# A hybrid mixer trunk on one core: a 128-column GLA state, norm factors spread by transposes, the heads' scale on the outputs, and the channel mixer's carry tile made last

## The chip, the cores and the metric

One Trainium2 chip, of which the kernel uses one core. The metric is the device time in microseconds of one execution. TensorE is called PE here, VectorE DVE, ScalarE ACT, GpSimdE POOL, and SyncE, which issues the DMAs, SP.

## The reference

One layer of a decoder trunk over 2048 tokens of width 1024, float32 throughout.

```python
def reference(x, c, ...):
    mod = silu(c) @ w_ada + b_ada                  # sh1, sc1, g1, sh2, sc2, g2
    h = rms_norm(x) * (1 + sc1) + sh1
    x = x + g1 * token_mixer(h)
    h = rms_norm(x) * (1 + sc2) + sh2
    x = x + g2 * conv_ffn(h)                       # up-projection, causal conv of width 3, silu gate, down-projection
    return rms_norm(x) * final_gain

def token_mixer(h):
    proj = h @ w_in                                # q, k, v and gates of three groups of heads
    o_r = rms_norm(retention(q_r, k_r, v_r)) * silu(gate_r)     # 4 heads, fixed decays
    o_h = rms_norm(gated_state(q_h, k_h, v_h, log_f)) * silu(gate_h)   # 8 HGRN2 heads, 64 keys each
    o_a = rms_norm(gated_state(q_a, k_a, v_a, g_log)) * silu(gate_a)   # 4 GLA heads, 32 keys each
    return (concat(o_r, o_h, o_a) * head_gain) @ w_out

# gated_state, in chunks: S is the state of one head (keys x 64 values)
#   o = attn @ v + (q * exp(cum)) @ S
#   S = exp(last) * S + (k * exp(last - cum)).T @ v
```

## The kernel before

The tokens are worked off in four blocks of 512, each of four chunks of 128 tokens. In a block the units run in the order h0, g, h1, h2, h3, r0, r1: two HGRN2 heads to each h, all four GLA heads in g (as two subs), two retention heads to each r. Each unit projects its q, k, v and gate out of h with float32 weights that are split into a high and a low half (three matmuls for one), builds the attention in seven levels (`gated`), copies, transposes k, updates its state and multiplies (`attn_out`). Each pair of heads' output is then transposed (`transposed`), and split into halves too. `out_half(b, 0)` multiplies the first four of these eight outputs with the out-projection at the end of the block; `out_finish(b - 1)` does the second four after unit h0 of the next block, and takes the second norm. This mixer takes the first 1290 us; then the channel mixer runs as up- and down-products over two halves of the tokens.

The order on PE is written out by hand: a clock in the program (`clock`, `adv`, `clock.at`) counts the PE time that each step is thought to take, and steps that fall due are put in between. The orders on DVE, ACT and SP come from a scheduler that goes by priorities (`tc.high_priority`) and by the program's order. Tiles come from rings of buffers: whoever takes a buffer again waits for its last reader.

What the change touches:
- `piece` brings in one 512 KB piece of weights: raw data into the ring `wraw` of two buffers (NRAW), a high half `whi` by ACT, a low half `wlo` by DVE. Low halves are written to a scratch in DRAM (`keep`) in block 0 and read back later. Pieces of the out-projection are multiplied by the heads' scale in this step (`gain`), in four parts of 256 columns, and for them the high half is kept and read back as well. The same two raw buffers also take the adaLN weights (`wada`), which DVE works off one at a time between the pieces (`ada`, from the list `later`).
- `rstd` spreads a norm factor, one number for each token, over all partitions: a matmul of the factor as a broadcast with the identity (`second`). The startup and the last norm have a copy of that line.
- `states` holds for each unit the states of five chunks, 128 columns wide with two heads on the block diagonal, but 64 wide for the GLA unit (i == 4), whose four heads stand on 32 partitions each, one above the other.
- `attn_out` adds, for each chunk, the two heads' attention times v (64 columns each) and q times the state. With `qn`, a copy of the two heads' q in one tile, that is one matmul of 128 columns; without it (GLA) each head's q, zero elsewhere (`new_qbd`, three buffers that POOL zeroes), is multiplied with the state on its own.
- `m_all` is the mask for the copies of levels 1 to 16.
- `halo` carries the last two columns of the convolution's input from one half of the tokens to the other; it is the first tile of the pool `gemm`.

In the rows below, names carry the block first: rhqh is the raw piece for the q of an HGRN2 unit, hhqh and lhqh its high and low half, pshfh and pshqh the projections into PSUM, ha the high and low halves of the normed input, xn its unsplit form, bcn the spread norm factor, og, oh, or the outputs of a unit, oTg, oTh, oTr their transposes, ath and qbh the attention and the q of an h unit, hwo and lwo a piece of the out-projection.

Of the kernel before, what the change touches and what calls it, by code (L numbers as in the profile page):

```python
# [9 lines left out]
F32 = mybir.dt.float32  # L10
F32R = mybir.dt.float32r
I32 = mybir.dt.int32
U32 = mybir.dt.uint32
AF = mybir.ActivationFunctionType
ALU = mybir.AluOpType
# [85 lines left out]
def trunk(ctx, tc, xT, vecs, cvec, cst, rope, msk, wada, win, walow, wgla, wout, wup, wdown, out):  # L101
# [41 lines left out]
    m_all = p1.tile([P, 448], U32, tag="msk", name="m_all")  # L143
# [68 lines left out]
    def piece(src, name, key, gain=None, ahead=50):  # L212
# [3 lines left out]
        with tc.high_priority(offset=ahead):  # L216
            hi = pw.tile([P, 1024], F32R, tag="whi", name="h" + name)
            lo = pw.tile([P, 1024], F32R, tag="wlo", name="l" + name)
            if key + "h" in kept:
                nc.sync.dma_start(hi[:].bitcast(F32), kept[key + "h"][:])  # L220
                nc.sync.dma_start(lo[:].bitcast(F32), kept[key + "l"][:])
                return hi, lo
            raw = pw.tile([P, 1024], F32, tag="wraw", name="r" + name, bufs=NRAW)
            nc.sync.dma_start(raw[:], src)
            if gain is None:
                S.copy(hi[:], raw[:])
                if key + "l" in kept:
                    nc.sync.dma_start(lo[:].bitcast(F32), kept[key + "l"][:])
                else:
                    V.tensor_tensor(lo[:], raw[:], hi[:], op=ALU.subtract)  # L230
                    keep(key + "l", lo[:])
            else:
                n = 1024 // len(gain)
                for i, g in enumerate(gain):
                    sl = slice(i * n, (i + 1) * n)
                    S.activation(hi[:, sl], raw[:, sl], AF.Copy, scale=g)
                for i, g in enumerate(gain):
                    sl = slice(i * n, (i + 1) * n)
                    V.scalar_tensor_tensor(lo[:, sl], raw[:, sl], g, hi[:, sl], op0=ALU.mult, op1=ALU.subtract)
                keep(key + "h", hi[:])  # L240
                keep(key + "l", lo[:])
# [76 lines left out]
    def rstd(acc, name, bc, then, bank=None, gap=4.5):  # L318
# [13 lines left out]
        def second(r):  # L332
            p = bank("bc" + name)
            for c in range(NCH):
                T.matmul(p[:, c * P:(c + 1) * P], r[:, c:c + 1].to_broadcast([P, P]), ident, start=True, stop=True)
            S.copy(bc, p[:])
            then()
# [38 lines left out]
    def startup():  # L376
# [48 lines left out]
        for c in range(NCH):  # L425
            T.matmul(ps[:, c * P:(c + 1) * P], r[:, c:c + 1].to_broadcast([P, P]), ident, start=True, stop=True)
# [87 lines left out]
    states = [p1.tile([P, NS, 64 if i == 4 else P], F32, tag=f"S{i}", name=f"S{i}") for i in range(7)]  # L514
    for i, st in enumerate(states):
        if i != 4:
            G.memset(st[:], 0.0)
# [37 lines left out]
    def transposed(b, pos, o, name):  # L555
# [5 lines left out]
        S.copy(oT[:, 0, :], ps[:])  # L561
        V.tensor_tensor(oT[:, 1, :], ps[:], oT[:, 0, :], op=ALU.subtract)
        oTs[b][pos] = oT

    def attn_out(name, b, attn, v, q, Sst, qn=None):

        ps = late_ps("o" + name)
        for c in range(NCH):
            oc = ps[:, c * P:(c + 1) * P]
            cs = slice(c * P, (c + 1) * P)  # L570
            inter = not (b == 0 and c == 0)
            both = inter and qn is not None
            st = Sst[:, (b * NCH + c) % NS, :]
            if both:
                T.matmul(oc, qn[:, cs], st, start=True, stop=False)
            for hh in range(2):
                oo = oc[:, hh * 64:hh * 64 + 64]
                T.matmul(oo, attn[:, (c * 2 + hh) * P:(c * 2 + hh + 1) * P], v[:, c, hh * 64:hh * 64 + 64],
                         start=not both, stop=hh == 1 if both else not inter)
                if inter and not both:  # L580
                    T.matmul(oo, q[:, hh, cs], st, start=False, stop=True)
# [16 lines left out]
    def gated(name, b, ui, pos, kq, decay, subs, qk, sel):  # L598
# [16 lines left out]
        for li, s in enumerate(LEVELS):  # L615
# [9 lines left out]
            with tc.high_priority(offset=CHAIN):  # L625
# [7 lines left out]
                for ps, at in zip(pss, attns):  # L633
# [5 lines left out]
                    else:  # L639
                        mk = m_all[:, li * 64:li * 64 + 64].rearrange("p (n s) -> p n s", s=s)  # L640
# [3 lines left out]
        qn = None  # L644
# [4 lines left out]
        with tc.high_priority(offset=CHAIN):  # L649
            S.copy(kT[:].rearrange("p c n -> p (c n)"), ps[:])  # L650
            if not two:
                q, rows = subs[0][:2]
                qn = late("qn" + name)
# [884 lines left out]
```

## Time and profile before

| | |
|---|---|
| runs | 3 |
| median, lowest, highest | 2593.47, 2592.66, 2594.07 us |
| span of the profiled execution | 2594.1 us, 0.6 above the median |
| busy: PE, DVE, ACT, POOL | 97%, 77%, 43%, 6% |
| DMA | 533.89 MB, 60.4% of the 16 engines' time |

The profile shows one execution by engine, line and time. A group's row gives the line, the engine, what is written and read, the shape, the count, and the durations; matmuls are pipelined, so what a matmul costs is read from the distance between starts, not from its duration. A timeline's row gives start and duration in us, and in brackets how long the engine was idle just before, and what released it. In the chain of work that ended last, each piece is followed back to what released it.

### The profile page before, as it was taken

What the parts mean: (1) busy time and instruction counts of PE and PEld (TensorE: products, weight loads), DVE (VectorE), ACT (ScalarE), POOL (GpSimd) and SP (SyncE); (2) the same over time, 40 slices, a digit from 0 to 9 for tenths busy, and PEclk for the clock granted to TensorE, in tenths of its full rate; (3) what the DMA queues carried; (4) which work ended last, traced back from release to release, by engine and by line L of the source; (5) the groups of instructions that cost most, each with busy time, mean ns of one, the idle gap of its engine ahead of it and who ended that gap; (6) DMA issues with size and microseconds to landing.
All of it is one profiled execution on the core that took longest, in us unless ns stands there. A gap on an engine that the chain in (4) does not pass through costs nothing.

```text
span 2594.1 us, 37215 instructions
## 1 busy us (share of the span) xinstructions
PE 2525.0 (97%) x13198; PEld 2141.8 (83%) x13198; DVE 1991.7 (77%) x3650; ACT 1116.4 (43%) x1898; POOL 144.6 (6%) x246
## 2 busy tenths in 40 slices
PE   5999999999999999999999999999999999999998
PEld 4798878998889888998778888878878888888887
DVE  8778986868778786887688888886677778778566
ACT  3333434433343234333254445455444455455442
POOL 1000010000000000000010000000000001010000
PEclk9999999999999999999999999999999999999999
DMA  8543556765687846887665444477675544447663
GB/s 302 194 156 131 213 215 225 276 214 179 218 311 262 294 166 222 298 280 252 204 233 173 149 144 161 146 268 242 204 228 167 154 143 145 154 132 258 207 188 126
DMA packets 232778, 533.89 MB, mean 206 GB/s; under 512 B 25072, under 2 KB 28176, under 8 KB 232592
## 3 DMA queue, kind: packets, MB, share of 16 engines
q1 hardware_dynamic: 232592, 531.52, 60.4%
q8 instruction: 104, 1.70, 0.3%
q14 instruction: 82, 0.67, 0.1%
HBM read 397.72 MB, written 133.69 MB: 205 GB/s over the span
## 4 chain that ended last, share of the span: by engine, by line
PE 85%; DVE 7%; DMA 4%; ACT 2%; issue 1%; SPq 0%; DVEq 0%; ACTq 0%
PE X L246 6%; PE X L248 6%; PE X L247 6%; PE lvh L622 3%; PE Z L247 3%; PE Z L246 3%; PE Z L248 3%; PE dX L248 3%; PE dX L246 3%; PE dX L247 3%; PE psqkvgr L248 2%; PE psqkvgr L246 2%; PE psqkvgr L247 2%; PE y L246 2%; PE y L248 2%; PE y L247 2%
## 5 line engine op out<-in xcount | busy, mean ns | idle before, releaser
L246 PE MATMUL X<-B,A 128*128 128x512 f32 x572 | 224.9, 393 | 1.4 <-ACT u L1245 1.4
L247 PE MATMUL X<-B,A 128*128 128x512 f32 x572 | 224.3, 392 | 0.3 <-DMA B<-made 0.2
L248 PE MATMUL X<-B,A 128*128 128x512 f32 x572 | 224.4, 392 | 0.0
L973 DVE TENSOR_TENSOR dA<-rd,dA 128x512 fp32r<-128x512 f32 x154 | 106.0, 689 | 94.4 <-ACT dA L972 93.9
L972 ACT CAST dA<-rd 128x512 fp32r<-128x512 f32 x154 | 95.4, 619 | 147.1 <-PE dY L248 47.3
L973 DVE TENSOR_TENSOR A<-s,A 128x512 fp32r<-128x512 f32 x176 | 120.4, 686 | 42.6 <-ACT A L972 42.4
L246 PE MATMUL psvgh<-hvgh,ha 128*128 128x256 f32 x480 | 140.3, 292 | 0.0
L248 PE MATMUL dX<-dB,dA 128*128 128x512 f32 x352 | 139.0, 395 | 0.0
L246 PE MATMUL dX<-dB,dA 128*128 128x512 f32 x352 | 139.0, 395 | 0.0
L247 PE MATMUL dX<-dB,dA 128*128 128x512 f32 x352 | 138.9, 395 | 0.0
L247 PE MATMUL psvgh<-lvgh,ha 128*128 128x256 f32 x480 | 136.0, 283 | 0.0
L248 PE MATMUL psvgh<-hvgh,ha 128*128 128x256 f32 x480 | 136.0, 283 | 0.0
L972 ACT CAST A<-s 128x512 fp32r<-128x512 f32 x176 | 108.3, 617 | 62.2 <-PE Z L248 47.5
L246 PEld LDWEIGHTS X<-B,A 128*128 128x128 f32 x572 | 107.7, 188 | 25.6 <-ACT u L1245 2.2
L247 PEld LDWEIGHTS X<-B,A 128*128 128x128 f32 x572 | 107.7, 188 | 24.4 <-DMA B<-made 1.3
L248 PEld LDWEIGHTS X<-B,A 128*128 128x128 f32 x572 | 107.6, 188 | 23.4
L246 PE MATMUL Z<-B,A 128*128 128x512 f32 x308 | 121.7, 395 | 2.3 <-ACT B L972 1.7
L622 PEld LDWEIGHTS lvh<-qbh,kh 128*128 128x128 f32 x896 | 115.8, 191 | 7.8 <-issue 1.4
L247 PE MATMUL Z<-B,A 128*128 128x512 f32 x308 | 121.5, 395 | 0.3 <-DVE B L973 0.3
L248 PE MATMUL Z<-B,A 128*128 128x512 f32 x308 | 121.6, 395 | 0.0
L622 PE MATMUL lvh<-qbh,kh 128*128 128x128 f32 x896 | 120.8, 277 | 0.3 <-DVE kh L632 0.3
L973 DVE TENSOR_TENSOR A<-r,A 128x512 fp32r<-128x512 f32 x130 | 89.3, 687 | 32.2 <-ACT A L972 32.2
(453 smaller groups left out, 7149.3 us busy)
## 6 DMA issues: line engine op xcount, KB each, us to landing
gs<-yv SPq DMA_DIRECT2D x154, 256.0 KB, 2.9
rb<-gs SPq DMA_DIRECT2D x154, 256.0 KB, 4.0
r<-wup SPq DMA_DIRECT2D x141, 256.0 KB, 3.3
s<-sumsu SPq DMA_DIRECT2D x132, 256.0 KB, 3.0
wada<-wada SPq DMA_DIRECT2D x48, 512.0 KB, 4.8
rd<-sumsd SPq DMA_DIRECT2D x88, 256.0 KB, 3.9
rd<-wdown SPq DMA_DIRECT2D x66, 256.0 KB, 3.7
x<-xT SPq DMA_DIRECT2D x64, 256.0 KB, 5.1
```

Source lines behind the costliest of these rows:

```text
L246: T.matmul(ps, lhs[0], rhs[0], start=first, stop=False, skip_group_check=more)
L247: T.matmul(ps, lhs[0], rhs[1], start=False, stop=False, skip_group_check=more)
L248: T.matmul(ps, lhs[1], rhs[0], start=False, stop=last, skip_group_check=more)
L622: T.matmul(ps[:, c * P:(c + 1) * P].rearrange("p (h n s) -> p h n s", h=2, s=s), kq[:, c * P:(c + 1) * P], rhs, start=True, stop=True)
L972: S.copy(hi, src)
L973: V.tensor_tensor(lo, src, hi, op=ALU.subtract)
```

## The change

- The GLA unit's state becomes 128 columns wide, with two heads on the block diagonal as for the other units, and is zeroed at the start. In `gated` the second head's q is copied beside the first one's in the same tile, for all units, and `attn_out` multiplies it with the state in one matmul of 128 columns. The tile `qn` of the h units is gone: their matmul reads q itself.
- The norm factors are spread by transposes in place of matmuls, in all three places.
- The out-projection's weights are no longer multiplied by the heads' scale. Its high halves are cast from raw in every block, like those of the other pieces, and only the low halves are kept. The scale goes onto the transposed outputs, where they are split.
- The mask is loaded as 256 columns and one column in sixteen of the next 64; level 16 reads that column as a broadcast.
- `halo` is made when it is first used, as the last tile of its pool.

```diff
@@ the mask
-    m_all = p1.tile([P, 448], U32, tag="msk", name="m_all")
+    m_all = p1.tile([P, 260], U32, tag="msk", name="m_all")
...
-    nc.sync.dma_start(m_all[:], msk)
+    nc.sync.dma_start(m_all[:, 0:256], msk[:, 0:256])
+    with nc.allow_non_contiguous_dma("one column in sixteen of the mask"):
+        nc.sync.dma_start(m_all[:, 256:260], msk[:, 256:320:16])
...
-                        mk = m_all[:, li * 64:li * 64 + 64].rearrange("p (n s) -> p n s", s=s)
+                        if s < 16:
+                            mk = m_all[:, li * 64:li * 64 + 64].rearrange("p (n s) -> p n s", s=s)
+                        else:
+                            mk = m_all[:, 256:260].unsqueeze(2).to_broadcast([P, nb, s])
@@ piece
-    def piece(src, name, key, gain=None, ahead=50):
+    def piece(src, name, key, ahead=50):
...
-            if key + "h" in kept:
-                nc.sync.dma_start(hi[:].bitcast(F32), kept[key + "h"][:])
-                nc.sync.dma_start(lo[:].bitcast(F32), kept[key + "l"][:])
-                return hi, lo
             raw = pw.tile([P, 1024], F32, tag="wraw", name="r" + name, bufs=NRAW)
             nc.sync.dma_start(raw[:], src)
-            if gain is None:
-                S.copy(hi[:], raw[:])
-                if key + "l" in kept:
-                    nc.sync.dma_start(lo[:].bitcast(F32), kept[key + "l"][:])
-                else:
-                    V.tensor_tensor(lo[:], raw[:], hi[:], op=ALU.subtract)
-                    keep(key + "l", lo[:])
+            S.copy(hi[:], raw[:])
+            if key + "l" in kept:
+                nc.sync.dma_start(lo[:].bitcast(F32), kept[key + "l"][:])
             else:
-                n = 1024 // len(gain)
-                for i, g in enumerate(gain):
-                    sl = slice(i * n, (i + 1) * n)
-                    S.activation(hi[:, sl], raw[:, sl], AF.Copy, scale=g)
-                for i, g in enumerate(gain):
-                    sl = slice(i * n, (i + 1) * n)
-                    V.scalar_tensor_tensor(lo[:, sl], raw[:, sl], g, hi[:, sl], op0=ALU.mult, op1=ALU.subtract)
-                keep(key + "h", hi[:])
+                V.tensor_tensor(lo[:], raw[:], hi[:], op=ALU.subtract)
                 keep(key + "l", lo[:])
@@ second, in rstd; the same line in startup and in the last norm
-                T.matmul(p[:, c * P:(c + 1) * P], r[:, c:c + 1].to_broadcast([P, P]), ident, start=True, stop=True)
+                T.transpose(p[:, c * P:(c + 1) * P], r[:, c:c + 1].to_broadcast([P, P]), ident)
@@ states
-    states = [p1.tile([P, NS, 64 if i == 4 else P], F32, tag=f"S{i}", name=f"S{i}") for i in range(7)]
-    for i, st in enumerate(states):
-        if i != 4:
-            G.memset(st[:], 0.0)
+    states = [p1.tile([P, NS, P], F32, tag=f"S{i}", name=f"S{i}") for i in range(7)]
+    for st in states:
+        G.memset(st[:], 0.0)
@@ transposed
-        S.copy(oT[:, 0, :], ps[:])
-        V.tensor_tensor(oT[:, 1, :], ps[:], oT[:, 0, :], op=ALU.subtract)
+        hg = vec[:, V_HG + pos:V_HG + pos + 1]
+        S.activation(oT[:, 0, :], ps[:], AF.Copy, scale=hg)
+        V.scalar_tensor_tensor(oT[:, 1, :], ps[:], hg, oT[:, 0, :], op0=ALU.mult, op1=ALU.subtract)
@@ attn_out
-    def attn_out(name, b, attn, v, q, Sst, qn=None):
+    def attn_out(name, b, attn, v, qn, Sst):
...
-            both = inter and qn is not None
-            st = Sst[:, (b * NCH + c) % NS, :]
-            if both:
-                T.matmul(oc, qn[:, cs], st, start=True, stop=False)
+            if inter:
+                T.matmul(oc, qn[:, c * P:(c + 1) * P], Sst[:, (b * NCH + c) % NS, :], start=True, stop=False)
...
-                if inter and not both:
-                    T.matmul(oo, q[:, hh, cs], st, start=False, stop=True)
@@ gated
             S.copy(kT[:].rearrange("p c n -> p (c n)"), ps[:])
-            if not two:
-                q, rows = subs[0][:2]
-                qn = late("qn" + name)
-                for hh, (r0, r1) in enumerate(rows):
-                        S.copy(qn[r0:r1, :], q[r0:r1, hh, :])
+            for q, rows, v, sg in subs:
+                r0, r1 = rows[1]
+                S.copy(q[r0:r1, 0, :], q[r0:r1, 1, :])
...
-                        es = slice(0, 64) if two else slice(64 * hh, 64 * hh + 64)
+                        es = slice(64 * hh, 64 * hh + 64)
...
-            ps = attn_out(f"{name}_{i}", b, at, v, q, Sst, qn)
+            ps = attn_out(f"{name}_{i}", b, at, v, q[:, 0, :], Sst)
@@ the gemm pool (halo[:, t, :] becomes halo(t) where it is used)
-    halo = pg.tile([P, 2 * NF + 4, 2], F32, tag="halo", name="halo")
+    halos = []
+
+    def halo(t):
+        if not halos:
+            halos.append(pg.tile([P, 2 * NF + 4, 2], F32, tag="halo", name="halo"))
+        return halos[0][:, t, :]
```

PE's order stays the same apart from the rows below. For GLA unit 0 of block 0 (og: its first output; S: the state, vg: v, atg: the attention, qbg: q) PE has before:

```order
L248 MATMUL psvgh_2_0_1572<-hvgh_2_1_1663,ha_7_636 128x256
L578 MATMUL og_0_1685<-vg_0_855,atg_0_1150 128x64 x3
L581 MATMUL og_0_1685<-S_111,qbg_0_848 128x64
L578 MATMUL og_0_1685<-vg_0_855,atg_0_1150 128x64
L581 MATMUL og_0_1685<-S_111,qbg_0_848 128x64
```

and after:

```order
L233 MATMUL psvgh_2_0_1572<-hvgh_2_1_1665,ha_7_637 128x256
L559 MATMUL og_0_1687<-vg_0_857,atg_0_1150 128x64 x2
L557 MATMUL og_0_1687<-S_111,qbg_0_850 128x128
L559 MATMUL og_0_1687<-vg_0_857,atg_0_1150 128x64 x2
L557 MATMUL og_0_1687<-S_111,qbg_0_850 128x128
L559 MATMUL og_0_1687<-vg_0_857,atg_0_1150 128x64 x2
```

Of the first chunk, which has no state yet, nothing changes; each later chunk has one matmul of 128 columns ahead of the two with v, in place of one of 64 behind each.

On DVE at the turn from block 0 to block 1 (wada: the adaLN weights that stand in a raw buffer; omsr, orsr, nw: the norm of unit r0 and its Newton steps; S_113: the state of unit r1), before, around the adaLN step and, some 60 rows later, around the last xn and ha:

```order
L352 SCALAR_TENSOR_TENSOR xn_1_2753<-xn_1_2753,mod,bc_1_1855 128x512
L197 ISA wada_3105,mod<-wada_3105,c_act,vec 128x1024
L197 ISA mod 128x1
...
L158 SCALAR_TENSOR_TENSOR orsr_0_3143<-nw,orsr_0_3143 128x8
L352 SCALAR_TENSOR_TENSOR xn_7_2789<-xn_7_2789,mod,bc_1_1855 128x512
L156 SCALAR_TENSOR_TENSOR nw<-orsr_0_3143 128x8
L562 TENSOR_TENSOR oTh_3_0_3162<-oTh_3_0_3157,oTh_3_0_3162 128x512
L157 TENSOR_TENSOR nw<-nw,omsr_0_3140 128x8
L197 ISA wada_3214,mod<-wada_3214,c_act,vec 128x1024
L197 ISA mod 128x1
L158 SCALAR_TENSOR_TENSOR orsr_0_3143<-nw,orsr_0_3143 128x8
L359 SCALAR_TENSOR_TENSOR ha_7_2792<-xn_7_2789,mod,ha_7_2792 128x512
```

and after:

```order
L337 SCALAR_TENSOR_TENSOR xn_6_2775<-xn_6_2775,mod,bc_1_1851 128x512
L337 SCALAR_TENSOR_TENSOR xn_7_2781<-xn_7_2781,mod,bc_1_1851 128x512
L843 TENSOR_TENSOR or_0_3094<-or_0_3082,c_all 128x512
L344 SCALAR_TENSOR_TENSOR ha_6_2778<-xn_6_2775,mod,ha_6_2778 128x512
L344 SCALAR_TENSOR_TENSOR ha_7_2784<-xn_7_2781,mod,ha_7_2784 128x512
L532 TENSOR_REDUCE omsr_0_3098<-osqr_0_3096 128x8
...
L822 SCALAR_TENSOR_TENSOR S_113<-S_113,c_all,ur_1_3138 64x64
L158 SCALAR_TENSOR_TENSOR orsr_0_3101<-nw,orsr_0_3101 128x8
L197 ISA wada_3063,mod<-wada_3063,c_act,vec 128x1024
L197 ISA mod 128x1
L156 SCALAR_TENSOR_TENSOR nw<-orsr_0_3101 128x8
```

The xn and ha steps for k = 7 have moved ahead of the norm and the state updates of the retention units, and the adaLN step, which stood right behind the xn step for k = 1, has moved behind them all; before, the next adaLN step (wada_3214) stood between the last xn and its ha.

On SP at the same turn (what a load waits for stands in the brackets: DMAHW is a queue's earlier transfer, the engines' names stand for a step of theirs), before:

```order
L224 DMA rhfh_0_3110<-win 128x1024 [waits DMAHW3_49]
L228 DMA lhfh_0_3109<-kepti1l 128x1024 [waits DMAHW4_49,PE_49]
L499 DMA xn_2_2759<-xT 128x512 [waits DMAHW5_49,DVE_49]
L499 DMA xn_3_2765<-xT 128x512 [waits DMAHW6_49,DVE_49]
L499 DMA xn_4_2771<-xT 128x512 [waits DMAHW7_49,DVE_49]
L190 DMA wada_3214<-wada 128x1024 [waits DMAHW3_49,DMAHW0_49,Activation_49]
L224 DMA rhqh_0_3219<-win 128x1024 [waits DMAHW1_49,DVE_49]
L228 DMA lhqh_0_3218<-kepti0l 128x1024 [waits DMAHW2_49,PE_49]
```

and after:

```order
L484 DMA xn_5_2769<-xT 128x512 [waits DMAHW7_49,DVE_49]
L484 DMA xn_6_2775<-xT 128x512 [waits DVE_49]
L223 DMA lhqh_0_3176<-kepti0l 128x1024 [waits DMAHW1_49,PE_49]
L484 DMA xn_7_2781<-xT 128x512 [waits DMAHW2_49,PE_49]
L223 DMA lvgh_0_0_3281<-kepti2l 128x1024 [waits DMAHW3_49,PE_49]
L223 DMA lvgh_0_1_3338<-kepti3l 128x1024 [waits DMAHW4_49,PE_49]
L220 DMA rhqh_0_3177<-win 128x1024 [waits DMAHW5_49,DVE_49]
L190 DMA wada_3277<-wada 128x1024 [waits DMAHW6_49,DVE_49]
L220 DMA rvgh_0_0_3282<-win 128x1024 [waits DMAHW7_49,DMAHW5_49,Activation_49]
```

The load of rhqh waits for DVE's adaLN step in both, since it takes that buffer; it has moved behind the loads of two low halves of v (lvgh), of which the second waits for PE to have read the low half of hfh. On ACT the cast of hhqh moves with it: before, it stood ahead of the ha steps for k = 5 and 6; after, it stands behind the two steps that read pshfh.

20 lines of the change are left out of this document (8 added, 12 removed).

## The prediction

> **What bounds the kernel now.** I read the page first (busy shares, the chain that ended last), then the PE waits, then the groups of instructions by line, and last the timeline and the windows round the places that the change touches.
>
> ```profile
> span 2594.1 us, 37215 instructions
> PE 2525.0 (97%) x13198; PEld 2141.8 (83%) x13198; DVE 1991.7 (77%) x3650; ACT 1116.4 (43%) x1898; POOL 144.6 (6%) x246
> PE 85%; DVE 7%; DMA 4%; ACT 2%; issue 1%; SPq 0%; DVEq 0%; ACTq 0%
> ```
>
> ```profile
> PE ssn L418 <- DVE san L346: 14.8, 1, 14.8
> PE X L246 <- ACT m L1232: 4.1, 1, 4.1
> ```
>
> PE is busy for 2525.0 of 2594.1 us and carries 85% of the chain, so what leaves PE's stream leaves the time, unless PE then stands waiting for something that did not become earlier. Its 69 us of idle time (2594.1 - 2525.0) are 14.8 us ahead of the first matmul and small gaps elsewhere; the waits, in total, times and longest, give 4.1 us as the largest of the second half. The profiled span is 0.6 us above the median of the runs, 2593.47; sums below are made against the span and 0.6 is taken off at the end. I count 0.2% (5.2 us) either way as no change, about what a measurement of this kernel can tell.
>
> **The change part by part.**
>
> The GLA state. The group's row and the timeline show what a pass costs:
>
> ```profile
> L581 PE MATMUL og<-S,qbg x120: 275/275/275, 177.6 to 1104.4; 128*128 128x64 f32 x120
> 177.62 0.39 PE L581 MATMUL og<-S,qbg 128*128 128x64 f32 x2
> 177.84 0.39 PE L578 MATMUL og<-vg,atg 128*128 128x64 f32 x2
> 178.06 0.39 PE L581 MATMUL og<-S,qbg 128*128 128x64 f32 x2
> 613.58 0.38 PE L575 MATMUL oh<-S,qnh 128*128 128x128 f32 x2
> 613.80 0.56 PE L578 MATMUL oh<-vh,ath 128*128 128x64 f32 x4
> ```
>
> Each matmul stands there as two records (two passes). Two 64-column passes take 0.22 us from start to start (177.62, 177.84, 178.06), and the two 128-column passes of the HGRN2 heads take the same 0.22 (613.58 to 613.80). A pass costs 0.112 us whatever its columns, so 120 passes of 64 columns turned into 60 of 128 save 60 x 0.112 = 6.7 us: 12 passes (1.3 us) in block 0, 16 (1.8 us) in each later block. The Trainium skill, in "TensorE: Matmul & The Clock Gate", section "Back-to-back issue gap", gives an isolated matmul of 1 to 64 columns about 60 cycles and one of 128 columns 134 cycles; by that table this part would save nothing. The same section says that weight loads set the pace too, and the rows, with equal steps for both widths, side with that; the table stays as a rival with a small chance.
>
> Norm factors. A transpose is one pass where the fp32 matmul is two:
>
> ```profile
> L335 PE MATMUL bcn<-c_all,rsn x80: 270/275/377, 217.3 to 2567.1; 128*128 128x128 f32 x80
> 217.33 1.16 PE L335 MATMUL bcn<-c_all,rsn 128*128 128x128 f32 x8 [0.29 <-DVE rsn L158]
> 218.24 0.36 PE L246 MATMUL psvgh<-hvgh,ha 128*128 128x256 f32 x1
> 280.71 0.44 PE oTh L559 x4
> 18.86 2.08 PE L426 MATMUL bcn<-c_all,rsn 128*128 128x128 f32 x8 [2.23 <-DVE rsn L158]
> 20.98 0.58 ACT L429 COPY bc<-bcn 128x512 f32<-128x512 f32 x1 [3.51 <-PE bcn L426]
> 2579.66 0.46 PE bcn L1340 x4
> 2586.50 1.24 PE bcn L1340 x4
> ```
>
> Eight passes take 0.91 us (217.33 to 218.24), 0.114 each; four transposes on the chain take 0.44, which is 0.11 each. L335 loses 40 of 80: 4.6 us. At the start the clock is cold: eight passes in 2.08 us, of which the last lasts some 0.4, so 0.23 a pass and 0.9 us for four, all of it on the path, since ACT waits for them (3.51) and PE's next matmul waits for ACT's product. At the end two groups of four passes become two each: 0.46 gives back 0.23, the cold 1.24 about 0.5, and DVE's last steps read both. Together 6.2 us, and with the state 12.9 us taken out of PE.
>
> Heads' scale. PE's work stays; the edit moves load between the others.
>
> ```profile
> 292.99 1.66 DVE L239 SCALAR_TENSOR_TENSOR lwo<-rwo,vec,hwo 128x256 fp32r<-128x256 f32 x4
> L226 ACT CAST hhqh<-rhqh x15: 1033/1054/1057, 119.2 to 1108.7; 128x1024 fp32r<-128x1024 f32 x15
> 233.24 1.22 DVE L305 TENSOR_TENSOR lqkvgr<-rqkvgr,hqkvgr 128x1024 fp32r<-128x1024 f32 x1
> 310.40 0.69 ACT L826 ACTIVATE qnr<-qTr,c_all 128x512 f32<-128x512 f32 x1
> 608.09 0.59 ACT L650 COPY kTh<-kTh 128x512 f32<-128x512 f32 x1 [1.73 <-PE kTh L647]
> 609.93 1.05 PE L661 MATMUL uh<-vh,kTh 128*128 128x128 f32 x8
> ```
>
> In block 0 a piece's four ACT parts become one cast of 1.05, and DVE's four (1.66) one subtraction of 1.22 (the shape of L305): 8 x 0.44 = 3.5 us less on DVE. The 32 transposed outputs take ACT's scaled form of 0.69 in place of the plain copy of 0.59, 3 us in all, and DVE's form with a scale. In blocks 1 to 3 the high half is no longer read back ready-made: 24 raw loads go through the ring of two raw buffers that the other pieces and the adaLN weights share, and 24 casts of 1.05 us go onto ACT, 25 us. ACT is busy 43%, so the sum does not matter, the place does: a cast ahead of a short copy that PE waits for. One now stands ahead of the kT copy of 608.09, ahead of which ACT was idle for 1.73 us. By the order of the loads I estimate its buffer to be full near 607.4, the cast to end near 608.5 and the copy near 609.1; PE needs it at 609.93: hidden by 0.8 us. So these casts cost between 0 (all like this one) and 12 x 1.05 = 12.6 us (each of the 12 in a block's last quarter exposed); by the nearest row it is the low end, and I take 1.0, one cast exposed. Less than 0 is possible in block 0 alone, where it is priced next. The eight write-backs of the high half go (4 of 533.89 MB), and at the mixer's end SP is no longer held by reloads.
>
> Block 0 to block 1. This is where the order on DVE, ACT and SP turns over.
>
> ```profile
> 285.50:327.00 41.50, 40.56 (x238) 35.30 (x236) 40.44 (x101) 19.33 (x37) 3.01 (x6) 1.00 0.59 210
> 331.40:336.20 4.80, 4.80 (x14) 3.81 (x12) 2.87 (x5) 2.13 (x3) 0.00 (x0) 0.50 0.90 335
> 301.39 1.28 DVE L197 CUSTOM_DVE_ANT_0 wada<-wada,c_act,vec 128x1024 f32<-128x1024 f32 x1
> 302.70 0.33 SPq L224 DMA_DIRECT2D rhqh<-win  x1
> 327.23 0.66 DVE xn L352
> 328.71 0.51 PE L246 MATMUL pshfh<-ha,hhfh 128*128 128x512 f32 x1 [2.64 <-ACT ha L356]
> 330.77 0.80 PE L247 MATMUL pshfh<-ha,hhfh 128*128 128x512 f32 x1 [1.56 <-DVE ha L359]
> 331.79 0.63 PE L246 MATMUL pshqh<-ha,hhqh 128*128 128x512 f32 x1
> rvgh<-win SPq DMA_DIRECT2D x30, 512.0 KB, 4.7
> ```
>
> In the windows' rows the columns are the window, its length, then busy time of PE, weight loads, DVE, ACT and POOL, the clock, DMA share and GB/s. DVE is busy for 40.44 of 41.5 us here, so its order decides. Before, PE stops twice for the last piece of ha (2.64 + 1.56 us) and then runs at half clock (0.50) until 336.2. After, the last xn and ha pieces move ahead, and I count ha ready 2 to 3 us before PE asks: that gap goes. But the adaLN step of 301.39 goes behind them and behind a row of state updates and Newton steps. It frees the raw buffer into which rhqh is loaded (302.70, right behind it). In the old order those Newton steps were past at 327.23, where DVE turns to the last xn. In the new one the xn and ha steps (about 0.66 each) stand ahead of them and the adaLN step (1.28) does not, which cancels; PE's earlier work takes off 2.7, and the adaLN step itself adds 1.28 less 0.4 for the shorter subtraction: near 325.4. SP has a second wait ahead of that load, for PE to finish pshfh (about 324.5). So: load issued near 325.4, 4.7 us to land, 1.05 to cast, PE starts pshqh near 331.1 instead of 331.79, after some 6.8 us of standing and with the clock cold as before. The 2.7 us saved up to there (0.9 at the start, 1.3 state, 0.46 one norm) end in this wait and 0.5 is kept. Bounds: PE starts no earlier than pshfh's end (324.3, 7 us better, excluded by the two waits) and, if DVE is not early at all, at 333.6 (2 us worse).
>
> Small edits. The second halves of q: h heads copy one half (0.62 us) instead of two, g heads gain eight copies where ACT stands idle, so nothing. But q is now held until PE has read it:
>
> ```profile
> 524.22 1.10 POOL L509 MEMSET qbr<- 64x512 f32 x2 [28.78 <-ACT qnh L655]
> 525.37 0.96 POOL L606 MEMSET ath<- 128x1024 f32 x1
> 535.81 0.44 PE L575 MATMUL oh<-S,qnh 128*128 128x128 f32 x2
> 540.22 1.31 DVE L641 COPY_PREDICATED ath<-m_all,lvh 128x512 f32<-128x512 uint32 x1
> ```
>
> POOL's zeroing of q then starts at 536.3 instead of 524.2, the zeroing of ath queued behind it ends at 538.3, and DVE writes into ath at 540.22: hidden by 1.9 us. One more state tile to zero and one more mask load lie at the start, under PE's 14.8 us; the load is some 0.3 us of issue more and the mask is first used long after. The carry tile made last shifts the second half's buffers; no row prices that, and the nearest is the wait of 4.1 us quoted first, the largest there: half of it either way, -2 to +2, and I take 0.
>
> Sum: 2594.1 - 12.9 + 2.7 (lost at the boundary) - 0.5 + 1.0 = 2584.4, and against the median 2583.8.
>
> **The rivals.**
> - *The raw ring stops PE again at later boundaries.*
>
> ```profile
> 625.88 1.05 ACT L226 CAST hhqh<-rhqh 128x1024 fp32r<-128x1024 f32 x1 [0.70 <-PE y L247]
> L246 PE MATMUL pshqh<-ha,hhqh x6: 389/389/393, 646.5 to 649.9; 128*128 128x512 f32 x6
> ```
>
> The stretch worked out above (PE standing 6.8 us, then 4.8 us at half clock, 2.4 lost) costs 9.2 us each time that a late raw buffer meets an idle ring. For it: two buffers, three more loads of the same size in each out-projection half, and covers of only 0.8 us. Against it: at the next boundary that cast runs at 625.88 and PE first uses it at 646.5 (the second row, of a window round there), 20 us later. It decides if a raw load lands more than 0.8 us later than I estimate ahead of the kT copy. One such stop gives 2593.0, no change; two or more 2602, slower.
> - *The block 0 boundary closes.* If rhqh's buffer came free in time, the 4.2 us of standing and 2.4 of cold clock would go and the 2.7 be kept: 2594.1 - 12.9 - 4.2 - 2.4 + 1.0 - 0.6 = 2575.0. The waits in the order speak against it.
> - *Columns, not passes, set the price.* Then the state's 5.4 us of blocks 1 to 3 are not gained: 2589.2, no change. The equal steps of 0.22 speak against it.
> - *The gain goes into waits that are there anyway.* Each block ends in DVE and ACT chains; should those not follow PE, half of the 10.2 us of the later parts stays: about 2588.9.
>
> **How the numbers follow.** Forecast 0.55, mostly 2579 to 2587; one more stop 0.17; two or more 0.08; boundary closed 0.07; columns 0.05; waits that are there anyway 0.08, half of it on each side of the 0.2% bound (2588.3). Faster: 0.55 + 0.07 + 0.04 = 0.66; same 0.17 + 0.05 + 0.04 = 0.26; slower 0.08. The range leaves out the two-stop case and most of the closed boundary: 2577 to 2593.5.
>
> **What would show it.** Right: the state's rows of og with 60 records and steps of 0.22; 40, 4 and 4 records for the norm factors; no wait for ha at 326, but one of 5 to 8 us of PE for the cast of hhqh, at half clock behind it; the timelines 10 us apart by 1300. Wrong: PE waits with a raw load or a cast as releaser near 630 to 670, 930 to 970 or 1245, a wait for ath's zeroing, or og's steps of 0.3.

## The result, and the profile after

Four runs of the changed kernel took 2567.62 to 2571.45 us, median 2569.32, beside 2593.06 for the kernel before (four runs, 2589.9 to 2594.07). The ratio is 0.991, with a 95% interval of 0.9896 to 0.9924. The gain is 23.7 us where 9.3 were forecast (2593.1 - 2583.8), and the time lies below the range. The profiled execution is the slowest of the four, 2571.45 us, with a span of 2569.7.

The page of the kernel after, its span and busy times:

```profile
span 2569.7 us, 36949 instructions
PE 2491.6 (97%) x13090; PEld 2124.7 (83%) x13090; DVE 1992.9 (78%) x3626; ACT 1134.6 (44%) x1890; POOL 144.6 (6%) x247
```

PE's busy time fell by 33.4 us, of which the parts that remove passes were to take 12.9. The rest left PE without any matmul leaving it: the surviving ones run closer together. At the same time PE's idle time rose from 69 to 78 us. Both are found by laying the two timelines over each other. The table gives the time of one and the same matmul of PE in the kernel before, and by how much it stands earlier in five other kernels (in us; the experiments are told below, "carry first" and "carry last" are the first two of them, "carry 512" is the third, and "q copied" stands among the other parts).

| time before, step | after | carry first | carry last | carry 512 | q copied |
|---|---|---|---|---|---|
| 218.24 psvgh, end of the units of block 0 | 2.9 | 4.4 | -0.5 | 5.4 | 2.3 |
| 331.79 pshqh, start of block 1 | 0.0 | 1.8 | -0.5 | 3.4 | 0.0 |
| 641.33 or | 4.5 | 5.4 | 0.8 | 6.9 | 5.1 |
| 1012.00 bcn | 1.3 | 3.1 | 1.2 | 4.5 | 5.7 |
| 1288.45 ssn, end of the token mixer | 2.8 | 5.0 | 1.8 | 7.2 | 9.1 |
| 1357.04 X | 6.8 | 8.7 | 3.0 | 10.8 | 13.5 |
| 1896.70 dY, end of the first half | 15.0 | 8.7 | 11.3 | 19.1 | 21.7 |
| 2586.50 bcn, last norm | 23.8 | 10.1 | 18.3 | 30.3 | 34.9 |

Each column is one execution, and PE's mean granted clock differs between them: 0.991 before and in carry first, 0.992 after and in carry last, 0.993 in carry 512 and q copied. A thousandth of 2594 us is 2.6 us, and single runs spread in this way: of ten runs of one kernel below (the state alone) the one at 0.995 took 2579.19 us and the one at 0.990 2591.57. In the built programs, after, carry first and carry 512 have the same order of instructions on every engine and differ in addresses, yet at 218 their leads are 2.9, 4.4 and 5.4: from 98 to 112 the clock was 0.88, 0.88 and 1.00, from 128 to 142 it was 0.88, 1.00 and 1.00. So 2 or 3 us between two columns show nothing by themselves.

In "after" 17 of the 23.8 us come behind 1357, in the channel mixer, where the prediction had next to nothing (0.23 us of a norm). They come at a steady pace, not at a wait. The windows' rows (window, length, then busy time and count of PE, weight loads, DVE, ACT, POOL, then the clock) show it at full clock with PE busy all the time. Before, in an up stage and in a down stage:

```profile
1400.00:1500.00 100.00, 100.00 (x439) 82.14 (x438) 82.13 (x104) 48.77 (x73) 7.64 (x21) 1.00 0.49 162
1750.00:1850.00 100.00, 100.00 (x430) 80.46 (x429) 66.09 (x105) 49.09 (x87) 0.00 (x0) 1.00 0.70 228
```

After:

```profile
1400.00:1500.00 100.00, 100.00 (x443) 82.81 (x442) 84.79 (x107) 50.94 (x74) 7.66 (x21) 1.00 0.49 156
1750.00:1850.00 100.00, 100.00 (x443) 82.81 (x442) 67.52 (x107) 50.28 (x89) 0.00 (x0) 1.00 0.70 227
```

443 matmuls of 512 columns run in 100 us, where there were 439 and 430. The step, the distance from the start of one to the start of the next, is now 0.2267 us for all of them. In the timeline before, three products of twelve matmuls each follow one another in an up stage; their starts are

```profile
1406.35 0.39 PE L246 MATMUL Y<-B,A 128*128 128x512 f32 x1
...
1409.07 0.40 PE L246 MATMUL X<-B,A 128*128 128x512 f32 x1
...
1411.86 0.40 PE L246 MATMUL Z<-B,A 128*128 128x512 f32 x1
...
1414.66 0.39 PE L246 MATMUL X<-hB,A 128*128 128x512 f32 x1
```

so Y takes 2.72 us (0.2267 a matmul), X 2.79 (0.2325) and Z 2.80 (0.2333), of the same shape, with no wait. The same X and Z after:

```profile
1401.96 0.39 PE L231 MATMUL X<-B,A 128*128 128x512 f32 x1
...
1404.68 0.39 PE L231 MATMUL Z<-B,A 128*128 128x512 f32 x1
...
1407.40 0.39 PE L231 MATMUL X<-hB,A 128*128 128x512 f32 x1
```

2.72 and 2.72. The slow products before are exactly those that read their moving tile B, or dB in the down stages, from the ring `hc`. That ring lies in the pool `gemm`, behind the carry tile.

The largest waits of PE after that differ from before (us in total, times, longest):

```profile
PE pshqh L231 <- ACT hhqh L221: 7.1, 1, 7.1
PE bcn L320 <- DVE rsn L158: 4.6, 6, 1.1
PE pshfh L231 <- ACT sgg L523: 4.2, 1, 4.2
```

The first is the forecast stop at the start of block 1. The second is a wait for the norm factors, and the kernel before has less of it:

```profile
PE pshfh L246 <- ACT sgg L539: 2.8, 1, 2.8
PE bcn L335 <- DVE rsn L158: 1.5, 3, 0.9
```

### The profile page after: what moved, and what is told of

Read it like the earlier page. It is cut to its first block, busy times and chain, and to the rows that moved or that the text cites. A ratio compares the mean times of both kernels' runs of the same rounds, so it can differ in the third digit from the quotient of the medians.

```text
span 2569.7 us, 36949 instructions
## 1 busy us (share of the span) xinstructions
PE 2491.6 (97%) x13090; PEld 2124.7 (83%) x13090; DVE 1992.9 (78%) x3626; ACT 1134.6 (44%) x1890; POOL 144.6 (6%) x247
## 4 chain that ended last, share of the span: by engine, by line
PE 83%; DVE 10%; DMA 4%; issue 1%; ACT 1%; SPq 0%; DVEq 0%; ACTq 0%
PE X L231 6%; PE X L233 6%; PE X L232 6%; PE lvh L601 3%; PE Z L231 3%; PE Z L232 3%; PE Z L233 3%; PE dX L233 3%; PE dX L231 3%; PE dX L232 3%; PE psqkvgr L231 2%; PE psqkvgr L233 2%; PE psqkvgr L232 2%; PE lvg L601 2%; PE psvgh L231 2%; PE psvgh L233 2%
## 5 line engine op out<-in xcount | busy, mean ns | idle before, releaser
L231 PE MATMUL dX<-dB,dA 128*128 128x512 f32 x352 | 136.9, 389 | 0.0
L232 PE MATMUL dX<-dB,dA 128*128 128x512 f32 x352 | 136.9, 389 | 0.0
L233 PE MATMUL dX<-dB,dA 128*128 128x512 f32 x352 | 136.9, 389 | 0.0
L951 DVE TENSOR_TENSOR dB<-rb,dB 128x512 fp32r<-128x512 f32 x154 | 105.3, 685 | 11.9 <-ACT dB L950 11.9
```

Source lines behind the costliest of these rows:

```text
L231: T.matmul(ps, lhs[0], rhs[0], start=first, stop=False, skip_group_check=more)
L232: T.matmul(ps, lhs[0], rhs[1], start=False, stop=False, skip_group_check=more)
L233: T.matmul(ps, lhs[1], rhs[0], start=False, stop=last, skip_group_check=more)
L951: V.tensor_tensor(lo, src, hi, op=ALU.subtract)
```

## Experiments

All times are medians, with lowest and highest run in brackets; the ratio is to the kernel before on the same chip. Where an expectation names a theory by a letter: A says that a moving tile which starts at a multiple of 512 bytes is slow; B, that the new order of buffers changes what is waited for; C, that fewer loads of the out-projection's weights are what helps; D, that the moving and the stationary tile have to start at the same place; E, that a tile's own place counts, whatever the other operand's; F, that each norm gives back 0.46 us to a wait; H, that POOL's later zeroing holds DVE; J, that the adaLN step on DVE makes the stop at the start of block 1. Other letters are rivals to these.

### The carry tile

**Carry last alone**, on the kernel before:

```diff
-    halo = pg.tile([P, 2 * NF + 4, 2], F32, tag="halo", name="halo")
+    def halo(t):                      # made at its first use, as in the change
```

> The kernel before with the carry tile made last, and nothing else of the change. The two traces show the second half's 512-column matmuls at 0.233 us where their moving tile comes from the channel mixer's own pool, against 0.2267 after. Theory A (addresses): the carry tile's 384 B in front put the pool's tiles at multiples of 512 B, last they stand 128 B past one, and that is worth 17 us from 1360 us on, and up to 4 in the stretch from 1290 to 1360: 2572 to 2576 us. Theory B (waits: another tile first means other releases to wait for) gives the same here, but without a change of the matmuls' steps. Theory C (fewer DMAs and less work of the out-projection's weights is what helps the second half): 2593 us, steps of 0.233 stay.

2576.01 us (2573.03 to 2581.04) beside 2593.6; ratio 0.9934 (0.9917 to 0.9952). This part alone is worth 17.6 us, and its steps are 0.2267 everywhere.

**Carry first again**, the other way round: the changed kernel with that one edit undone.

> The changed kernel with the carry tile first again. Theories A and B: the 17 to 21 us come back, 2586 to 2590 us, with steps of 0.233 in the same products as before. Theory C: 2569 us, steps of 0.2267.

2585.08 us (2581.9 to 2585.3), ratio 0.9963 (0.995 to 0.9976): everything but the carry tile is worth 8.5 us. The slow steps are back:

```profile
1750.00:1850.00 100.00, 100.00 (x431) 80.43 (x430) 66.16 (x105) 49.45 (x87) 0.00 (x0) 1.00 0.69 220
```

From 1357 to 2547 its lead stays between 8.5 and 10.0 us.

**Carry first, but 512 bytes long.** The order of the buffers is that of before; only what lies behind the carry tile moves by 128 bytes.

```diff
-    halo = pg.tile([P, 2 * NF + 4, 2], F32, tag="halo", name="halo")
+    halo = pg.tile([P, 64, 2], F32, tag="halo", name="halo")
```

> The changed kernel with the carry tile first again, but made 512 B long instead of 384, so that the tiles behind it start 128 B past a multiple of 512 as in the changed kernel. Theory A: 2569 us, steps of 0.2267. Theory B: as with the carry tile first, 2586 to 2590 us. Theory C: 2569 us.

2566.15 us (2564.94 to 2567.16), ratio 0.9896 (0.9879 to 0.9912), and 443 matmuls again:

```profile
1750.00:1850.00 100.00, 100.00 (x443) 82.81 (x442) 69.59 (x110) 51.98 (x92) 0.00 (x0) 1.00 0.69 223
```

So neither the order nor a wait does it, and the order of instructions is the same on every engine. The 384 bytes of the carry tile do: they push the ring `hc`. In the built program before, 2772 of the channel mixer's 5412 matmuls of 512 columns read `hc`. In the trace their mean step is 0.2329 us, against 0.2267 after; 2772 x 0.0062 is 17.2 us, about all that the carry tile is worth. Before, `hc` starts at a multiple of 512 bytes within a partition, and after at 128 bytes past one. The other operand, a split tile in an earlier pool, stands at 128 past in both.

**An unused tile in front of the pool**, of 128, 64 or 256 bytes, on the changed kernel:

```diff
+    front = pg.tile([P, 32], F32, tag="front", name="front")     # 16 and 64 in the other two
+    nc.gpsimd.memset(front[:], 0.0)
```

> The changed kernel with an unused tile of 128 B (zeroed once by POOL) ahead of the pool's tiles, which then start 256 B past a multiple of 512; the stationary tiles stay at 128 past. If only a start at a multiple of 512 is slow (theory A): 2569 us, steps of 0.2267. If what counts is that moving and stationary tile stand at the same offset (theory D): steps of 0.23 or more, 2580 to 2590 us.

2581.05 us (2578.05 to 2583.94), ratio 0.9952 (0.9937 to 0.9967). `hc` now starts at 256 past a multiple of 512, and its products are slow:

```profile
1750.00:1850.00 100.00, 100.00 (x430) 80.42 (x430) 66.97 (x105) 49.33 (x87) 0.00 (x0) 1.00 0.69 220
```

Theory A, that only multiples of 512 are slow, falls.

> The changed kernel with 64 B ahead of the pool's tiles, which then start 192 B past a multiple of 512 (the weights at 128), so 64 B off theirs. Theory D: steps above 0.2267 in the products whose moving tile stands in that pool. Theory E: 0.2267, since 192 is no multiple of 256.

One run, 2575.53 us. `hc` at 192; steps of 0.229 to 0.231 in its products, between the two:

```profile
1750.00:1850.00 100.00, 100.00 (x439) 82.05 (x438) 66.99 (x105) 49.74 (x88) 0.00 (x0) 1.00 0.69 224
```

> The changed kernel with 256 B ahead of the pool's tiles, which then start 384 B past a multiple of 512 (the weights at 128). If the offset counts within 256 B: steps of 0.2267 and about 2569 us; if it counts within 512 B or more (theory D in its narrow form): 0.233 and about 2581 to 2586 us. Theory E: 0.2267.

One run, 2569.11 us. `hc` at 384; all steps 0.2267:

```profile
1750.00:1850.00 100.00, 100.00 (x443) 82.81 (x442) 67.50 (x107) 50.63 (x89) 0.00 (x0) 1.00 0.70 226
```

**All at 0.** The mask is cut to 156 columns and 384 bytes of room go in front of the constants, so that both operands start at multiples of 512 bytes:

```diff
+    room = pc.tile([P, 96], F32, tag="room", name="room")        # ahead of vec
-    m_all = p1.tile([P, 260], U32, tag="msk", name="m_all")
+    m_all = p1.tile([P, 156], U32, tag="msk", name="m_all")      # one column in s for levels 4, 8 and 16
```

> The changed kernel with 384 B of unused room at the start of SBUF's constants, so that the weights, the normed inputs, the other rings and the channel mixer's pool all start at multiples of 512 B; the mask is kept in fewer columns (one in s for the levels 4, 8 and 16) to make room. With the pool at 0 and at 256 past while the weights stood at 128, steps were 0.233, with both at 128 0.2267. Theory D (moving and stationary tile must stand at the same offset): steps of 0.2267 everywhere, 2569 us within some 4. Theory E (a moving tile at a multiple of 256 is slow, wherever the weights stand): every 512-column matmul of the second half takes 0.233, some 4700 of them by 6.5 ns, 2600 us or more.

2567.02 us (2564.61 to 2570.59), ratio 0.99 (0.9867 to 0.9933):

```profile
1750.00:1850.00 100.00, 100.00 (x442) 82.79 (x442) 69.76 (x110) 52.07 (x93) 0.00 (x0) 1.00 0.69 223
```

`hc` starts at a multiple of 512, as before, and is fast. Theory E falls too, and theory D holds, counted within 256 bytes: what counts is how the two operands stand to each other:

| kernel | moving tile, stationary tile (bytes past a multiple of 512) | apart, modulo 256 | step |
|---|---|---|---|
| before, carry first | 0, 128 | 128 | 0.2325 to 0.2333 |
| front 128 | 256, 128 | 128 | 0.2325 to 0.2333 |
| front 64 | 192, 128 | 64 | 0.229 to 0.231 |
| after, carry last, carry 512 | 128, 128 | 0 | 0.2267 |
| front 256 | 384, 128 | 0 | 0.2267 |
| all at 0 | 0, 0 | 0 | 0.2267 |

The stationary tile stood only at 128 or at 0 in these kernels, and only three distances were tried; a rule by the sum of the two places would fit the rows as well. What in the chip makes this so stays open.

### The other parts

**Transposes alone**, the three lines of the norm factors, on the kernel before:

> The kernel before with the norm factors spread by transposes and nothing else. By the prediction's sum 6.2 us of PE leave. Theory F (a PE that comes earlier to the next norm waits for DVE's factor, so each later norm gives its 0.46 back): 2590 to 2593 us, with waits of about 0.4 us more ahead of the transposes than before. Theory G (the waits ahead of the norm factors in the changed kernel, 1 us each, come from the state's part, not from this): the full 5 to 6 us, 2587 to 2588.

2590.51 us (ten runs, 2585.39 to 2598.73) beside 2592.65; ratio 0.9986 (0.997 to 1.0003), so by time alone it is not told from no change. The interval holds the 6.2 us that were forecast as well as nothing. The profiled execution does not decide it: its lead is 4.0 us at 1288 and 8.1 at the last norm, but its clock was 0.994 against 0.991, which is worth some 7 us. The time lies in the range of theory F; but the waits of its norms hardly grow, which speaks against the reason that F gives:

```profile
PE bcn L335 <- DVE rsn L158: 1.9, 3, 0.9
```

**State alone**, on the kernel before: 128 columns of state and the second half of q copied for GLA, the smaller mask (without which there is no room), but `qn` kept for the h units.

> The kernel before with the GLA state of 128 columns (and the mask in 260 columns, which makes the room), q of the HGRN2 heads still copied. 60 passes of 0.112 us less: 2586.5 us if all of it comes through, og's steps 0.22 for two passes; about 2590 if PE's earlier arrival turns into waits at the block boundaries; 2593 if columns set the price.

2583.45 us (ten runs, 2579.19 to 2591.57) beside 2593.6; ratio 0.9966 (0.9952 to 0.9979), which is 5 to 12 us and holds the 6.7 forecast. PE keeps its lead at the start of block 1 (3.9 us at 218 and at 331.79), as it does with the transposes alone (3.5 at both): neither brings the stop there. Of what is left, the carry tile alone does not bring it, and with q copied it stays (the table). So it comes with the heads' scale, or with several parts together; the scale was not run alone.

**q copied.** The changed kernel, with the h units' q copied out to a tile of its own again:

```diff
-            for q, rows, v, sg in subs:
-                r0, r1 = rows[1]
-                S.copy(q[r0:r1, 0, :], q[r0:r1, 1, :])
+            # for GLA as in the change; for the h units:
+                qn = late("qn" + name)
+                for hh, (r0, r1) in enumerate(rows):
+                    S.copy(qn[r0:r1, :], q[r0:r1, hh, :])
```

What it tests stands in the timeline of the kernel after. When block 1 ends, POOL zeroes q as soon as PE has read it, and then ath; DVE meanwhile takes the norm of unit h0's output (omsh), and PE's next norm factor (bcn) waits behind it:

```profile
693.81 1.09 POOL L494 MEMSET qbh<- 64x512 f32 x2 [57.11 <-PE oh L557]
694.96 1.85 POOL L585 MEMSET atg<- 128x1024 f32 x2
695.57 0.69 DVE L532 TENSOR_REDUCE omsh<-osqh 128x8 f32<-128x512 f32 x1 [0.76 <-ACT osqh L530]
696.29 1.44 DVE L533 TENSOR_SCALAR omsh<-omsh 128x8 f32<-128x8 f32 x1
696.75 0.96 POOL L585 MEMSET ath<- 128x1024 f32 x1
701.42 0.62 PE L320 MATMUL bcn<-c_all,rsn 128*128 128x128 f32 x4 [1.06 <-DVE rsn L158]
```

A DVE step of 8 columns takes 1.44 us and ends (697.73) with POOL's zeroing (697.71). Its group in the source view (shortest, median, longest in ns) shows that 0.164 is usual; twice more, at 394 and 1005, it takes 1.1 and 1.45 and ends with a zeroing of ath:

```profile
L533 DVE TENSOR_SCALAR omsh<-omsh x16: 155/164/1445, 119.5 to 1224.9; 128x8 f32<-128x8 f32 x16
```

Before, ACT's copy to `qn` released q 3.4 us earlier on the clock, POOL was done by 694.27, and none of the sixteen is long:

```profile
690.38 1.09 POOL L509 MEMSET qbh<- 64x512 f32 x2 [49.13 <-ACT qnh L655]
693.31 0.96 POOL L606 MEMSET ath<- 128x1024 f32 x1
```

```profile
L549 DVE TENSOR_SCALAR omsh<-omsh x16: 156/164/209, 120.6 to 1227.4; 128x8 f32<-128x8 f32 x16
```

> The changed kernel with q of the HGRN2 heads copied into a tile of its own again (two copies of a half on ACT), so that POOL may zero q's buffer before PE has read the product with the state. In the changed kernel three of DVE's small steps (scale and offset of a unit's mean square, 0.16 us) last 1.09 to 1.45 us and end with POOL's zeroing. Theory H (the zeroing, 7 us later than before, holds DVE in the chain of the block's norm, and PE waits for the factor): the three steps are back at 0.17, the waits of about 1 us ahead of the spread factors at 398, 701 and 1010 us shrink or go, some 2 to 3 us in all: 2566 to 2567 us. Rival I (PE waits since it comes earlier, DVE's step is by the way): waits stay, 2569 us.

2562.27 us (2560.35 to 2565.33) beside 2593.6; ratio 0.9883 (0.9864 to 0.9903). It has the lowest median of all that were run, 7 us below the changed kernel (which was timed on another occasion, beside 2593.06). The long steps and the wait for bcn are gone:

```profile
688.26 0.96 POOL L585 MEMSET ath<- 128x1024 f32 x1
695.20 0.17 DVE L533 TENSOR_SCALAR omsh<-omsh 128x8 f32<-128x8 f32 x1
699.18 0.60 PE L320 MATMUL bcn<-c_all,rsn 128*128 128x128 f32 x4
```

```profile
L533 DVE TENSOR_SCALAR omsh<-omsh x16: 157/165/220, 120.2 to 1220.0; 128x8 f32<-128x8 f32 x16
```

Theory H holds for the steps and the waits; the gain is larger than the 2 to 3 us that it foresaw. The Trainium skill, in "SBUF — State Buffer", section "Who interferes with whom", says that a tensor_scalar can run in a mode that takes the port pair which DVE shares with GpSimd, that the pair is held for a whole instruction, and that a tensor_reduce never contends. The trace agrees: the TENSOR_REDUCE of 695.57 takes its usual 0.69 beside POOL's zeroing, the TENSOR_SCALAR behind it stands until the zeroing is over. That it stood through the zeroing of ath too, which began 0.46 us after it, does not follow from the rule, and no row shows the mode that DVE ran in.

The three waits of PE behind these steps (0.99, 1.06 and 1.05) are 3.1 of the 7 us. In the table the lead over "after" is 4.4 us by 1012 and 6.3 by 1288: the wait for sgg is shorter too (3.42 us instead of 4.22), and one of 0.96 us ahead of a norm at 1286 is gone. The other 4.8 of the 11.1 us at the last norm cannot be put down to q: the profiled executions are the slowest run of one kernel and the fastest of the other, and 4.4 of them come between 1890 and 1934, where both do the same work. There PE waits 1.20 and 3.87 us after, 0.37 and 2.57 with q copied, and runs at half clock for longer behind the longer waits.

**The adaLN step at a higher priority**, on the changed kernel:

```diff
         if later:
-            ada(later.pop(0))
+            with tc.high_priority(offset=200):
+                ada(later.pop(0))
```

> The changed kernel with the adaLN steps at a higher priority, so that the first of block 1 stands ahead of the xn and ha steps on DVE again and the load of rhqh follows hfh's cast. Theory J (the 7.1 us stop ahead of pshqh comes from that step's place): no wait of PE for the cast of hhqh; the last ha is late again instead, as before (4.2 us in two waits), and PE is some 2 to 3 us further at 345 us: 2566 to 2567 us. Rival K (the raw ring of two buffers is short anyway, with 24 loads more): a wait for a cast of about the same length stays, 2569 us or more.

The stop at the start of block 1 is gone; PE waits 1.79 us for ha instead, and starts pshqh at 327.14:

```profile
326.56 0.50 PE L233 MATMUL pshfh<-ha,hhfh 128*128 128x512 f32 x1 [1.79 <-DVE ha L345]
327.14 0.39 PE L232 MATMUL pshqh<-ha,hhqh 128*128 128x512 f32 x1
```

after, that was

```profile
331.81 0.79 PE L231 MATMUL pshqh<-ha,hhqh 128*128 128x512 f32 x1 [7.10 <-ACT hhqh L221]
```

So theory J holds for the stop: the place of the adaLN steps, of which one holds the raw buffer, makes it (the edit raises them all). The time does not show the 4.7 us: 2570.47 (2559.67 to 2573.58, four runs), ratio 0.9907 (0.9879 to 0.9934). The profiled execution is the fastest of the four, at a clock of 0.994 where the others had 0.990 to 0.992, so whether those lose the gain again later stays open. Even in the fastest, PE waits longer for norm factors (4.6 us in all after):

```profile
PE bcn L321 <- DVE rsn L158: 6.0, 6, 2.5
```

**Both**, q copied and the priority:

> Both edits together: the changed kernel with q copied and the adaLN steps ahead. If theories H and J hold and add up, 4 to 6 us less than the changed kernel: 2563 to 2565 us. If either falls, 2566 to 2569.

2565.43 us (2562.65 to 2565.75), ratio 0.9892 (0.9874 to 0.9911). The two do not add up. The profiled execution leads by 14.6 us at 641, against 5.1 for q copied alone, and has 6.1 left at 1012. Some 6 us go at one place: PE waits 2.09 us there for a norm factor (bcn at 828.00) and then runs at half clock, where with q copied alone it waits 0.91 us and keeps the full clock. The two rows, this kernel and q copied alone:

```profile
828.00:842.00 14.00, 13.93 (x64) 13.47 (x65) 7.77 (x21) 1.59 (x5) 0.00 (x0) 0.51 0.31 111
834.00:848.00 14.00, 13.38 (x95) 12.35 (x96) 12.83 (x38) 2.88 (x6) 0.00 (x0) 1.00 0.64 223
```

## Why the prediction was wrong, step by step

**The failed step: the carry tile.** "The carry tile made last shifts the second half's buffers; no row prices that, and the nearest is the wait of 4.1 us quoted first, the largest there: half of it either way, -2 to +2, and I take 0." It is worth 17.6 us alone, and some 15.8 on top of the other parts (2585.08 - 2569.32, timed on two occasions). The mistake was to look for its price among the waits. Here a shift of addresses alone changed the step of 2772 matmuls, and the trace before had the sign of it: X and Z at 1409.07 and 1411.86 took 2.79 and 2.80 us where Y just ahead took 2.72. Twelve equal matmuls with two durations and no wait between them asked for a reason. The range, made of waits and order alone, could not hold the result.

**The rest, in total: right, in part by luck.** Without the carry tile the forecast of 2583.8 met 2585.08. But the state alone took off as much (10.2 us) as everything but the carry tile (8.5): the other parts together, from which the sum had 3.0 us, gave nothing that the runs show.

**The state: right.** In the kernel after, a chunk's S and v matmuls stand

```profile
176.40 0.44 PE L557 MATMUL og<-S,qbg 128*128 128x128 f32 x2
176.68 0.56 PE L559 MATMUL og<-vg,atg 128*128 128x64 f32 x4
177.07 0.44 PE L557 MATMUL og<-S,qbg 128*128 128x128 f32 x2
```

0.67 us from chunk to chunk (176.40 to 177.07), for six passes. Before, eight passes, two rows of S and two of v, took 0.89, from 177.62 (a row of the prediction) to

```profile
178.51 0.39 PE L581 MATMUL og<-S,qbg 128*128 128x64 f32 x2
```

Two passes fewer, 0.22 less: the pass, not the column, is the price for these 64 and 128 columns, and the rival by which nothing would be saved falls.

**The norm factors: counts right, waits missed.** The rows count 40, 4 and 4 records, and the spread at the start takes 1.12 us instead of 2.08:

```profile
L320 PE MATMUL bcn<-c_all,rsn x40: 270/272/322, 215.0 to 2543.8; 128*128 128x128 f32 x40
L1325 PE MATMUL bcn<-c_all,rsn x4: 270/346/476, 2556.2 to 2563.0; 128*128 128x128 f32 x4
18.33 1.12 PE L411 MATMUL bcn<-c_all,rsn 128*128 128x128 f32 x4 [2.23 <-DVE rsn L158]
```

But PE now waits four times for a norm factor from DVE behind block 0 (0.99, 1.06, 0.85 and 1.05 us), where before it did so once for that long (0.89); three of the four are by the collision above. What the transposes alone gained, 2.1 us, is not told from nothing or from 6.2.

**q held longer: the second failed step.** It asked who reads the zeroed ath (DVE, 1.9 us later) and found cover. It did not ask what else DVE does in those microseconds while POOL writes. Undoing it gained some 7 us, of which three waits of PE are 3.1.

**Block 0 to block 1: right.** PE stops for 7.10 us (6.8 forecast) for the cast of hhqh and starts at 331.81 (331.1 forecast), and the lead of 2.9 us at 218 has become 0.0. The chain is the one forecast, on DVE, SP and ACT:

```profile
325.32 1.28 DVE L197 CUSTOM_DVE_ANT_0 wada<-wada,c_act,vec 128x1024 f32<-128x1024 f32 x1
326.63 0.33 SPq L220 DMA_DIRECT2D rhqh<-win  x1
330.71 1.04 ACT L221 CAST hhqh<-rhqh 128x1024 fp32r<-128x1024 f32 x1 [4.82 <-DMA rhqh<-win]
```

The sum had the adaLN step done and the load issued near 325.4; the step began then, so the load was issued 1.2 us later than forecast, and it landed in 4.1 us where 4.7 were taken. The two errors partly cancel.

**Later boundaries: no stop by the raw ring**, as forecast; the casts cost nothing that a wait shows. **The timelines 10 us apart by 1300: wrong.** They were 2.8 apart at 1288 (5.0 with the carry first, in the same order of instructions). Besides the norms, the wait for sgg grew from 2.8 to 4.2 us. In the first 70 us of the channel mixer 3.9 us came back that I had not priced. Before, Z waited 1.71 us for B, and PE's clock was 0.89 in the stretch behind it:

```profile
1304.36 0.51 PE L246 MATMUL Z<-B,A 128*128 128x512 f32 x1 [1.71 <-ACT B L972]
1304.36:1320.00 15.64, 15.34 (x58) 12.12 (x59) 14.04 (x23) 9.44 (x16) 0.64 (x1) 0.89 0.77 287
```

After, the wait is short and the clock stays:

```profile
1298.95 0.50 PE L231 MATMUL Z<-B,A 128*128 128x512 f32 x1 [0.58 <-ACT B L950]
1298.95:1314.60 15.65, 14.91 (x61) 11.25 (x62) 14.85 (x23) 10.96 (x19) 0.64 (x1) 1.00 0.88 321
```

So the total of the rest was met partly because misses cancel: less at 1288 than forecast, more behind it.

## What to carry to other kernels

Before pricing a change that moves buffers, compare the distance between starts of equal matmuls, product by product; where it differs without a wait, look at the addresses. Here PE was fastest when the moving and the stationary tile started a multiple of 256 bytes apart, and a tile of 384 bytes in front of one pool cost 0.7%. Before reading a few microseconds out of two single executions, compare their granted clocks. And where a buffer is released later, look not only at who needs it next but at which small DVE steps will then run beside POOL's zeroing.

## What the runs showed of the hardware

A matmul of 512 columns on one half of a split float32 operand (one pass) steps at 0.2267 us when its two operands' tiles start 0 or 256 bytes apart (modulo 512), at 0.229 to 0.231 when 64 apart, and at 0.2325 to 0.2333 when 128 apart. With unsplit float32 operands, eight passes of 64 columns took 0.89 us, and six, two of them of 128 columns, 0.67: 0.11 a pass in both. A DVE step of 0.16 us lasted up to 1.45 us beside a POOL zeroing. Behind a wait of 2.09 us PE's clock was 0.51 for 14 us, behind one of 0.91 at the same place it was full. Each was seen in this kernel alone.
